# Moving the tiles at the upper end of SBUF by 416 bytes, padding the rows of the transform operands, and keeping the probability tiles 32 bytes off

## The chip, the cores and the metric

The kernel runs on one core of one Trainium2 chip. The metric is the device time of one execution in microseconds; the time before is the median of three runs, and one more execution was taken with the profiler.

## The reference, cut to what matters

Two sequences (`x_prompt`, `x_sample`) of 1024 tokens, 1024 wide, go through one layer, all in float32. Each token row is normalised and modulated, then projected once; four heads of latent attention and eight groups of a two-dimensional Fourier transform share that projection and one output projection. A SwiGLU network of width 2816 follows.

```python
def layer(x, c, ...):
    h = rmsnorm(x, g_mix) * (1.0 + sc1) + sh1
    z = h @ w_in
    q_lat, kv_lat, k_pe, f_in = z[..., :o1], z[..., o1:o2], z[..., o2:o3], z[..., o3:]
    y_mla = mla_group(q_lat, kv_lat, k_pe, g_q_lat, w_uq, g_kv_lat, w_ukv)
    y_four = fourier_group(f_in, w_four)
    mix = jnp.concatenate([y_mla, y_four], axis=-1) @ w_out
    x = x + ga1 * mix
    h2 = rmsnorm(x, g_ffn) * (1.0 + sc2) + sh2
    ffn = (jax.nn.silu(h2 @ w_gate) * (h2 @ w_up)) @ w_down
    return x + ga2 * ffn
```

The result of each sequence is `rmsnorm(layer(x, c), g_final)`.

## The kernel before, in words

**The split product.** Nearly every product of two float32 matrices is made of three TensorE matmuls. Each operand is cut into a high part in the type float32r and the remainder: `split` (L63, L64) writes the high part with ScalarE and the remainder with VectorE. `mm3` (L79 to L81) then issues three matmuls into the same accumulator:

```python
nc.tensor.matmul(out, lh, rh, ...)   # L79
nc.tensor.matmul(out, lh, rl, ...)   # L80
nc.tensor.matmul(out, ll, rh, ...)   # L81
```

The second argument is the stationary operand, 128 columns that are loaded into the array by a weight load of its own (PEld in the profile); the third is the moving operand, up to 512 columns that stream past it. While one matmul streams, the weights of the next are loaded: at 999.85 us of the span a matmul of L81 starts, at 999.86 us the weight load for the L79 that follows it. So TensorE reads two places of SBUF at a time, the moving operand of this matmul and the stationary operand of the next. In the profile a group `bank<-H,wl` names what goes in, in no fixed order of moving and stationary; the lines settle it.

**The stages, in order of time.** First the input projection and the modulation vectors; then the Fourier transform, with moving `wm` and `wn` and stationary `A`, `B` and `ny` (`dft` and `fourier_out`, L946 to L1046; `wm` and `wn` are weights, `A` and `B` the transforms over the sequence). Then attention, in items of one sequence s, one block b of 256 rows, one head h and one half u: `scores` (L1216 to L1220) streams `lat`, the stored latents of sequence s, past `qa` and `qp`; the probabilities `p` are turned by transposes (`flip_p`, L1244) and split into `pt`; `values` streams `pt`, 256 columns wide, past `ckv`; `out_proj` streams `wv` past `o`. The items run s = 0 first, then s = 1, and the same code serves both.

Then the SwiGLU network, one sequence after the other, with a seven-product scheme for two-by-two blocks. **Gate and up** (`prod` and `step`): for each of 22 column blocks seven products, each of four chunks of 128, each of three matmuls. The moving operand is `H`, the normalised input in high and low parts, which stays in SBUF; the stationary one is `wh` and `wl`, split from the weights as they arrive. That is 22 x 7 x 4 = 616 calls of `mm3` for one sequence, 1232 for both. **Down** (`prod2`): the moving and the stationary operand are both fresh splits, so both are `wh` and `wl` tiles; 572 calls of `mm3` in this form. The last product of the second sequence is made from splits that were prepared in the room of the old `H` tiles, so there both operands are called `H`: 44 calls.

**Where the tiles lie.** A tile pool takes room from the lower end of each SBUF partition or, with `side="right"`, from the upper end; a pool is closed and its room is used again. The pools at the upper end grow down from byte 229344 of the partition, which is 32 more than a multiple of 64. What is in them comes in rows whose sizes are multiples of 64, so almost everything there starts 32 bytes off a multiple of 64, while the pools at the lower end start on multiples of 64. The starts, in bytes from the beginning of the partition as the built program has them, are these (a slice of a tile that the matmuls use starts a multiple of 512 bytes later, except in `A` and in the input projection's `wcs`):

| tile | end | part it plays | start before | rest by 64 | start after | rest by 64 |
|---|---|---|---|---|---|---|
| `H` (first of them `H20`) | lower | moving in gate and up | 11840 | 0 | 11840 | 0 |
| `wh` | upper | stationary in gate and up; both in down | 151520 | 32 | 151104 | 0 |
| `wl` | upper | the same | 176096 | 32 | 175680 | 0 |
| `val` | upper | sums, products, sources of `split` | 202720 | 32 | 202304 | 0 |
| `lat` of s = 0 | lower | moving in scores | 69184 | 0 | 69184 | 0 |
| `lat` of s = 1 | upper | moving in scores | 106464 | 32 | 105984 | 0 |
| `qa` | lower | stationary in scores | 42560 | 0 | 42560 | 0 |
| `qp` | lower | stationary in scores | 24128 | 0 | 24128 | 0 |
| `p` | upper | stationary in L1244 (`ident`, rest 0, moves) | 94176 | 32 | 93696 | 0 |
| `pt` | upper | moving in `values` | 122848 | 32 | 122400 | 32 |
| `ckv` | lower | stationary in `values` | 48704 | 0 | 48704 | 0 |
| `wv` | upper | moving in `out_proj` | 155616 | 32 | 155200 | 0 |
| `o` | upper | stationary in `out_proj` | 188384 | 32 | 187968 | 0 |
| `B` | upper | stationary in the Fourier stage (its `wm` stays at 32) | 107200 | 0 | 106720 | 32 |

All `wh`, `wl` and `val` tiles have the rest that the table gives for the first, and so have all `H` tiles.

Of the kernel before, what the change touches and what calls it, by code (L numbers as in the profile page):

```python
# [12 lines left out]
F32 = mybir.dt.float32  # L13
F32R = mybir.dt.float32r
# [7 lines left out]
P = 128  # L22
# [20 lines left out]
NZC = NCOS + NNYQ  # L43
NZS = 256
NCS = NZC + NZS
NY2 = 2 * NNYQ
ZOW = 4
NTE = 258
NT = 514
NX = 2 * (NCOS + NNYQ)  # L50


@with_exitstack
def hybrid_encoder_kernel(ctx: ExitStack, tc: tile.TileContext, a: dict):
# [4 lines left out]
    def rd(t):  # L59
        return t.bitcast(F32)  # L60

    def split(hi, lo, src, eng=None):
        here["a"] = nc.scalar.copy(hi, src).ins  # L63
        here["v"] = (eng or nc.vector).tensor_tensor(out=lo, in0=src, in1=rd(hi), op=ALU.subtract).ins  # L64
# [18 lines left out]
    const = ctx.enter_context(tc.tile_pool(name="const", bufs=1))  # L83
    tiny = ctx.enter_context(tc.tile_pool(name="tiny", bufs=4))
    dram = ctx.enter_context(tc.tile_pool(name="dram", bufs=1, space=DRAM))

    ident = const.tile([P, P], F32, name="ident")
    make_identity(nc, ident)
# [65 lines left out]
    zp = zpool.enter_context(tc.tile_pool(name="zp", bufs=1, side="right", reuse_waits="tile"))  # L154
    zc = [zp.tile([P, 4, NZC], F32, name=f"zc{s}") for s in range(2)]
    zs = [zp.tile([P, 4, NZS], F32, name=f"zs{s}") for s in range(2)]
    zo = zp.tile([ZOW, NZC], F32, name="zo")
    zx = zp.tile([P, NX], F32, name="zx")
    nc.gpsimd.memset(zx, 0.0)

# [3 lines left out]
    with ExitStack() as st:  # L164
        p1b = st.enter_context(ExitStack())
        w2 = p1b.enter_context(tc.tile_pool(name="p1b", bufs=1, side="right", reuse_waits="tile"))
        w = st.enter_context(tc.tile_pool(name="p1", bufs=1, reuse_waits="tile"))
# [568 lines left out]
        def raw_tile(name):  # L736
            return wr.tile([P, NT], F32, tag="raw", name=name, bufs=8)

        for _ in range(8):
            raw_tile("raw")  # L740
        zxs = [wr.tile([P, NX], F32R, name=f"zx{i}") for i in range(2)]
        zn = [wr.tile([P, 4, NY2], F32R, name=f"zn{i}") for i in range(2)]
        tcor = wr.tile([P, NTE], F32R, name="tcor")
        tb[0] = [wr.tile([P, 2, NT], F32R, name=f"tb0{i}") for i in range(2)]
        raws = {}

        def table_load(k):
            for c in range(2):
                raws[k, c] = raw_tile("raw")
                nc.sync.dma_start(raws[k, c][:, : (NT, 512)[k]], a[("tcos", "tsin")[k]][:, c, :])  # L750

# [64 lines left out]
    S = {}  # L816
# [98 lines left out]
    with ExitStack() as st:  # L915
        early = st.enter_context(ExitStack())
        wa = early.enter_context(tc.tile_pool(name="p2a", bufs=1, reuse_waits="tile"))
        w = st.enter_context(tc.tile_pool(name="p2", bufs=1, side="right", reuse_waits="tile"))
        pp = st.enter_context(tc.tile_pool(name="p2_ps", bufs=1, space=PSUM, reuse_waits="tile"))

        def bank2(tag="b"):
            return pp.tile([P, 512], F32, tag=tag, name="bank", bufs=2 if tag == "d" else 6)
# [5 lines left out]
            bank2(tag)  # L928

        zh, wms = {}, {}  # L930
        nyt = w.tile([P, NT], F32R, name="ny")
        for i in range(2):
            w.tile([P, 2, 512], F32R, tag=f"wm{i}10", name=f"wm{i}10", bufs=1)
        w.tile([P, 512], F32R, tag="wn1", name="wn1", bufs=1)
        nc.gpsimd.tensor_scalar(out=nyt, in0=ident[:, 0:1].broadcast_to([P, NT]), scalar1=0.0, scalar2=None, op0=ALU.mult).ins

# [8 lines left out]

        def dft(s, mid=None):  # L946
            z = zh.pop(s)
            A = [w.tile([P, 2, NT], F32R, tag=f"A{i}", name=f"A{i}", bufs=1) for i in range(2)]
            B = [w.tile([P, 2, 512], F32R, tag=f"B{i}", name=f"B{i}", bufs=1) for i in range(2)]
            if s == 0:  # L950
                wn0 = prep_wn(0, 0, wm1[1])
                next(wn0)
            for q in (0, 2, 1) if s == 0 else (0, 1):
                m = NY2 if q == 2 else P
                sl = slice(P * q, P * q + P)
                zz = zn if q == 2 else [z[0][i][:, :, sl] for i in range(2)]
                x0 = 2 * NCOS if q == 2 else NCOS * s + P * q
                pe, po = (bank2("d" if q == 0 else "b") for _ in range(2))
                for c in range(2):
                    mm3(pe[:m, :NTE], zz[0][:, 2 * c, :], zz[1][:, 2 * c, :], tb[0][0][:, c, :NTE], tb[0][1][:, c, :NTE], c == 0, False)  # L960
                for c in range(2):
                    mm3(po[:m, :256], zz[0][:, 2 * c + 1, :], zz[1][:, 2 * c + 1, :],
                        tb[0][0][:, c, NTE:NT], tb[0][1][:, c, NTE:NT], c == 0, c == 1)
                for i in range(2):
                    nc.tensor.matmul(pe[:m, :NTE], zxs[i][:, x0 : x0 + m], tcor, start=False, stop=i == 1)
                if q == 2:
                    ah = w.tile([NY2, NT], F32R, name="nyh")
                    al = raw_tile("nyl")[:NY2]
                else:
                    ah, al = A[0][:, q, :], A[1][:, q, :]  # L970
                for o, v in ((slice(0, 256), pe[:m, :256]), (slice(256, 512), po[:m, :256]), (slice(512, 514), pe[:m, 256:NTE])):
                    split(ah[:, o], al[:, o], v)
                if q == 2:
                    nc.vector.tensor_scalar(out=al, in0=al, scalar1=cmask[:m, 1:2], scalar2=None, op0=ALU.mult)
                    nc.vector.scalar_tensor_tensor(out=nyt[:m], in0=rd(ah), scalar=cmask[:m, 0:1], in1=al,
                                                   op0=ALU.mult, op1=ALU.add)
            if s == 0:
                with behind():
                    here["ny"] = here["a"], here["v"]
                    halves = [wm0, wm_half(0, 0, 1, w, wm1[0])]  # L980
                    wms[0] = {0: (halves, next(wn0))}
            if mid:
                mid()
            for q in range(2):
                sl = slice(P * q, P * q + P)
                pb = bank2()
                for v in range(2):
                    ks = slice(256 * v, 256 * v + 256)
                    for c in range(2):
                        mm3(pb[:, ks], z[1][0][:, 2 * c + v, sl], z[1][1][:, 2 * c + v, sl],  # L990
                            tb[1][0][:, c, ks], tb[1][1][:, c, ks], c == 0, c == 1)
                split(B[0][:, q, :], B[1][:, q, :], pb)
            return A, B, nyt

        def prep_wn(s, g, wnr):
            wnh = w.tile([P, 512], F32R, tag="wnh", name="wnh", bufs=1)
            wn = w.tile([P, 512], F32R, tag=f"wn{g}", name=f"wn{g}", bufs=1)
            nc.scalar.copy(wnh, wnr)
            nc.gpsimd.tensor_tensor(out=wnr, in0=wnr, in1=rd(wnh), op=ALU.subtract)
            nc.gpsimd.tensor_scalar(out=wnr, in0=wnr, scalar1=cmask[:, 3 + 2 * s : 4 + 2 * s], scalar2=None, op0=ALU.mult)  # L1000
            yield
            nc.vector.scalar_tensor_tensor(out=wn, in0=rd(wnh), scalar=cmask[:, 2 + 2 * s : 3 + 2 * s], in1=wnr,
                                           op0=ALU.mult, op1=ALU.add)
            yield wn
# [17 lines left out]
        def fourier_out(s, ABn, j, g):  # L1022
            A, B, ny = ABn
            (wc, wd), wn = wms[s][g]
# [3 lines left out]
            for q in range(2):  # L1028
                mm3(pa, A[0][:, q, js], A[1][:, q, js], wc[0][:, q, :], wc[1][:, q, :], q == 0, False)
            nc.tensor.matmul(pa, ny[:, js], wn, start=False, stop=True)  # L1030
# [7 lines left out]
            if j == 0:  # L1038
                pn = bank2()
                for q in range(2):  # L1040
                    mm3(pn[:2, :], A[0][:, q, 512:514], A[1][:, q, 512:514], wc[0][:, q, :], wc[1][:, q, :], q == 0, False)
                nc.tensor.matmul(pn[:2, :], ny[:, 512:514], wn, start=False, stop=True)
# [159 lines left out]
    with ExitStack() as st:  # L1202
        w = st.enter_context(tc.tile_pool(name="p3", bufs=1, side="right", reuse_waits="tile"))
# [32 lines left out]
        def flip_p(s, b, h, u):  # L1236
            p = S.pop(("p", s, b, h, u))
            if u == 0:
                S["pt", s, b, h] = [w.tile([P, 8, 2, P], F32R, tag=f"pt{k}", name=f"pt{k}", bufs=2) for k in range(2)]
            pth, ptl = S["pt", s, b, h]  # L1240
            for g in range(2):
                pt = tbank("ppt")
                for c in range(4):
                    nc.tensor.transpose(pt[:, c, :], p[:, (4 * g + c) * P : (4 * g + c + 1) * P], ident)  # L1244
                split(pth[:, 4 * g : 4 * g + 4, u, :], ptl[:, 4 * g : 4 * g + 4, u, :], pt)
# [18 lines left out]
        def comb_h(s, c):  # L1264
            A = e.tile([P, 4, 512], F32, tag="lat00", name="hca")
            B = e.tile([P, 4, 512], F32, tag="lat01", name="hcb")
# [51 lines left out]
        for k in range(nit + 4):  # L1318
            if k >= nit:
                i = k - nit  # L1320
# [5 lines left out]
            if k < nit:  # L1326
# [3 lines left out]
                i = k % 8  # L1330
# [27 lines left out]
    with ExitStack() as st:  # L1358
        w = st.enter_context(tc.tile_pool(name="p5", bufs=1, reuse_waits="tile"))
# [162 lines left out]
        for s in range(2):  # L1522
# [78 lines left out]
            A = {}  # L1601
            late = None
            for n, f in enumerate(order):
# [78 lines left out]
                if n % 2 == 1:  # L1682
                    late = (n // 2, A)
                    A = {}
# [300 lines left out]
```

## Time and profile before

| | |
|---|---|
| runs | 2051.56, 2048.66, 2051.51 us; median 2051.51 us |
| profiled execution | 2051.31 us |
| its span, first to last instruction | 2049.5 us, so 1.8 us lie around it |
| TensorE busy | 2006.0 us, 98% of the span |
| granted TensorE clock, mean | 0.996 |

How to read it: the profile's page names a group of instructions by line, engine, operation and tiles, with the count, the busy time and the mean length of one. The length of a matmul in the records reaches from the start of its stream to a modelled end; consecutive matmuls overlap, so the time that each one takes out of the span is the distance between two starts, which the timeline shows.

### The profile page before, as it was taken

Reading aid. Unit: us, or ns where it says so; the run is one execution under the profiler, and the core shown is the slowest. Engines: PE = TensorE matmul, PEld = TensorE weight load, DVE = VectorE, ACT = ScalarE, POOL = GpSimd, SP = SyncE. Lnnn points to the kernel's source line nnn. Section 1 sums busy time; section 2 is a strip of 40 time slices with the busy share of each in tenths; the row PEclk is TensorE's granted clock in tenths of the full one; section 3 lists DMA queues with packets and bytes.
Section 4 is the critical chain, followed back from the end, with each engine's and each line's share of the span. In section 5 each row is a group of like instructions: output and inputs, shape, how many; then the busy total and the mean of one; then the engine's idle time right before and its main releaser. Section 6 shows DMA issues by size and latency. Waiting matters only on the chain.

```text
span 2049.5 us, 28369 instructions
## 1 busy us (share of the span) xinstructions
PE 2006.0 (98%) x9910; PEld 1641.6 (80%) x9910; DVE 1397.2 (68%) x2076; ACT 890.5 (43%) x1732; POOL 827.0 (40%) x972
## 2 busy tenths in 40 slices
PE   7899999999999999999999999999999999999998
PEld 3778778888888878888888888877888888888876
DVE  4568758666677778767777577688665665667585
ACT  2675436555555563333232365454323333336441
POOL 0564213112313237878878311234544444420142
PEclk9999999999999999999999999999999999999999
DMA  9786884444544475555455587674322322258662
GB/s 387 256 317 211 293 307 116 111 99 113 146 102 143 139 268 202 174 194 186 174 172 186 168 305 249 216 233 162 132 93 88 117 90 103 94 182 277 221 231 95
DMA packets 183036, 376.64 MB, mean 184 GB/s; under 512 B 17996, under 2 KB 57548, under 8 KB 179052
## 3 DMA queue, kind: packets, MB, share of 16 engines
q1 hardware_dynamic: 165548, 321.33, 45.9%
q0 software_dynamic: 17344, 53.49, 8.7%
q8 instruction: 78, 1.28, 0.2%
q14 instruction: 66, 0.54, 0.1%
HBM read 262.75 MB, written 120.39 MB: 187 GB/s over the span
## 4 chain that ended last, share of the span: by engine, by line
PE 55%; DVE 3%; DMA 2%; issue 1%; POOL 1%; ACT 0%; SPq 0%; DVEq 0%; ACTq 0%; POOLq 0%
PE bank L81 18%; PE bank L79 18%; PE bank L80 18%; DVE wl L64 1%; DVE val L137 1%; DMA draw<-s_d 1%; POOL val L137 0%; DMA val<-x_d 0%; DVE val L1782 0%; DMA draw<-t_d 0%; ACT wh L63 0%; DVE val L134 0%; POOL rs_y L105 0%; DVE H L64 0%; DMA rgu<-in_wgu_dram 0%
## 5 line engine op out<-in xcount | busy, mean ns | idle before, releaser
L79 PE MATMUL bank<-H,wh 128*128 128x512 f32 x1232 | 487.5, 396 | 2.4 <-DVE val L137 0.9
L81 PE MATMUL bank<-H,wl 128*128 128x512 f32 x1232 | 488.6, 397 | 0.2 <-DVE wl L64 0.2
L80 PE MATMUL bank<-H,wh 128*128 128x512 f32 x1232 | 484.4, 393 | 0.3 <-DVE H L64 0.3
L79 PEld LDWEIGHTS bank<-H,wh 128*128 128x128 f32 x1232 | 231.2, 188 | 58.6 <-DVE val L137 1.8
L80 PEld LDWEIGHTS bank<-H,wh 128*128 128x128 f32 x1232 | 231.3, 188 | 58.1 <-DVE H L64 0.6
L81 PEld LDWEIGHTS bank<-H,wl 128*128 128x128 f32 x1232 | 231.3, 188 | 56.9 <-DVE wl L64 0.5
L64 DVE TENSOR_TENSOR wl<-draw,wh 128x512 fp32r<-128x512 f32 x286 | 202.7, 743 | 85.6 <-ACT wh L63 85.2
L137 DVE TENSOR_TENSOR val<-bank,val 128x512 f32<-128x512 f32 x200 | 136.7, 689 | 158.8 <-PE bank L81 153.4
L63 ACT CAST wh<-draw 128x512 fp32r<-128x512 f32 x286 | 168.6, 619 | 159.3 <-PE bank L80 82.9
L137 POOL TENSOR_TENSOR val<-val 128x512 f32<-128x512 f32 x58 | 84.0, 1456 | 365.5 <-DVE val L1756 188.8
L80 PE MATMUL bank<-wl,wh 128*128 128x512 f32 x572 | 223.6, 391 | 2.3 <-DVE wl L64 2.3
L63 ACT CAST wh<-rgu 128x512 fp32r<-128x512 f32 x172 | 106.8, 621 | 269.5 <-PE bank L80 209.5
L81 PE MATMUL bank<-wh,wl 128*128 128x512 f32 x572 | 222.6, 389 | 0.0
L79 PE MATMUL bank<-wh 128*128 128x512 f32 x572 | 222.6, 389 | 0.0
L63 ACT CAST wh<-val 128x512 fp32r<-128x512 f32 x133 | 82.2, 621 | 269.8 <-PE bank L80 253.1
L64 DVE TENSOR_TENSOR wl<-val,wh 128x512 fp32r<-128x512 f32 x133 | 130.8, 985 | 77.3 <-ACT wh L63 77.3
L64 DVE TENSOR_TENSOR wl<-rgu,wh 128x512 fp32r<-128x512 f32 x172 | 166.8, 970 | 3.7 <-ACT wh L63 3.7
L134 POOL TENSOR_TENSOR val<-rgu 128x512 f32<-128x512 f32 x80 | 117.7, 1472 | 100.9 <-DMA rgu<-in_wgu_dram 97.2
L80 PEld LDWEIGHTS bank<-wl,wh 128*128 128x128 f32 x572 | 107.3, 188 | 27.4 <-DVE wl L64 5.4
L79 PEld LDWEIGHTS bank<-wh 128*128 128x128 f32 x572 | 107.4, 188 | 22.4
L81 PEld LDWEIGHTS bank<-wh,wl 128*128 128x128 f32 x572 | 107.4, 188 | 22.2
L1225 DVE TENSOR_REDUCE mx<-ps_s 128x1 f32<-128x1024 f32 x64 | 78.2, 1222 | 61.3 <-PE ps_s L1220 60.9
(385 smaller groups left out, 4048.4 us busy)
## 6 DMA issues: line engine op xcount, KB each, us to landing
rgu<-in_wgu_dram SPq DMA_DIRECT2D x86, 512.0 KB, 4.4
draw<-s_d SPq DMA_DIRECT2D x143, 256.0 KB, 3.8
s_d<-val POOLq DMA_DIRECT2D x88, 256.0 KB, 3.9
draw<-t_d SPq DMA_DIRECT2D x88, 256.0 KB, 4.2
s_d<-val SPq DMA_DIRECT2D x66, 256.0 KB, 2.4
draw<-in_w_down_dram SPq DMA_DIRECT2D x55, 256.0 KB, 4.6
wada<-in_w_ada_dram SPq DMA_DIRECT2D x11, 1024.0 KB, 10.5
xt<-in_x_dram SPq DMA_DIRECT2D x16, 512.0 KB, 10.3
```

The costliest lines, as they stand in the source:

```text
L63: here["a"] = nc.scalar.copy(hi, src).ins
L64: here["v"] = (eng or nc.vector).tensor_tensor(out=lo, in0=src, in1=rd(hi), op=ALU.subtract).ins
L79: nc.tensor.matmul(out, lh, rh, start=first, stop=False, skip_group_check=cont)
L80: nc.tensor.matmul(out, lh, rl, start=False, stop=False, skip_group_check=cont)
L81: here["t"] = nc.tensor.matmul(out, ll, rh, start=False, stop=last, skip_group_check=cont).ins
L134: return eng.tensor_tensor(out=out, in0=x, in1=y, op=ALU.subtract).ins
L137: eng.tensor_tensor(out=out, in0=x, in1=y, op=ALU.add)
L1225: nc.vector.tensor_reduce(out=mx, in_=ps, axis=AX.X, op=ALU.max)
```

## The change

- A tile `edge` of 104 floats (416 bytes) in a pool of its own is taken first at the upper end. No instruction touches it. Every later pool at the upper end starts 416 bytes lower, an odd multiple of 32.
- `zo` gets 8 more floats behind its row, so what is allocated below it in the first stages moves by 448 bytes, a multiple of 64, and keeps its rest.
- `ny`, `A` and `nyh` get rows of 528 instead of 514 floats (2112 bytes, a multiple of 64, instead of 2056); the instructions use the first 514, as before.
- Before the first pair of `pt` tiles a tile of 32 bytes is allocated, and another after it, so that `pt` keeps its rest of 32 and the tiles behind it come to rest 0.

No instruction is added, removed or put elsewhere: TensorE has the same 8932 rows in the same order before and after, VectorE the same 1682, and so on for each engine. The waits are the same as well, but for one: the fill of `ny` on GpSimd no longer waits for an earlier matmul, since its new place doesn't overlap what that matmul read.

```diff
+NTP = 528
...
+    edge = ctx.enter_context(tc.tile_pool(name="edge", bufs=1, side="right"))
+    edge.tile([P, 104], F32, name="edge")
...
-    zo = zp.tile([ZOW, NZC], F32, name="zo")
+    zo = zp.tile([ZOW, NZC + 8], F32, name="zo")[:, :NZC]
...
-        nyt = w.tile([P, NT], F32R, name="ny")
+        nyt = w.tile([P, NTP], F32R, name="ny")[:, :NT]
...
-            A = [w.tile([P, 2, NT], F32R, tag=f"A{i}", name=f"A{i}", bufs=1) for i in range(2)]
+            A = [w.tile([P, 2, NTP], F32R, tag=f"A{i}", name=f"A{i}", bufs=1)[:, :, :NT] for i in range(2)]
...
-                    ah = w.tile([NY2, NT], F32R, name="nyh")
+                    ah = w.tile([NY2, NTP], F32R, name="nyh")[:, :NT]
...
             if u == 0:
+                if not S.get("gap"):
+                    w.tile([P, 8], F32, name="gap0")
                 S["pt", s, b, h] = [w.tile([P, 8, 2, P], F32R, tag=f"pt{k}", name=f"pt{k}", bufs=2) for k in range(2)]
+                if not S.get("gap"):
+                    S["gap"] = w.tile([P, 8], F32, name="gap1")
```

## The prediction

> **What bounds the kernel now.** First the page: the share of each engine, and the clock in 40 slices.
>
> ```profile
> span 2049.5 us, 28369 instructions
> ...
> PE 2006.0 (98%) x9910; PEld 1641.6 (80%) x9910; DVE 1397.2 (68%) x2076; ACT 890.5 (43%) x1732; POOL 827.0 (40%) x972
> ...
> PEclk9999999999999999999999999999999999999999
> ```
>
> TensorE has hardly a gap and its clock is full all along. A busy TensorE is not yet one that works at its best, so the next question is how far apart its matmuls stand. Before that, the stages: three stretches cut out of gate and up of the first sequence, down of the first, and gate and up of the second. Columns: length, busy time and count for PE, PEld, DVE, ACT and POOL, granted clock, DMA share, GB/s.
>
> ```profile
> 780.00:1180.00 400.00, 400.00 (x1716) 321.75 (x1716) 283.97 (x287) 121.59 (x204) 301.37 (x274) 1.00 0.52 178
> 1200.00:1410.00 210.00, 208.56 (x915) 171.03 (x914) 156.06 (x231) 110.34 (x205) 43.16 (x56) 1.00 0.71 239
> 1430.00:1830.00 400.00, 399.51 (x1713) 321.11 (x1712) 239.97 (x290) 122.28 (x206) 181.16 (x156) 1.00 0.30 105
> ```
>
> In gate and up TensorE is busy for 400.00 of 400 us and 399.51 of 400, with VectorE at 284 and 240 and GpSimd at 301 and 181. Nothing but TensorE sets the length of these stages. Now the groups by form: gate and up (`H` with `wh` or `wl`), down (`wh` and `wl` alone, two of its three lines), and the last product of down, where both operands are `H`.
>
> ```profile
> L81 PE MATMUL bank<-H,wl 128*128 128x512 f32 x1232 | 488.6, 397 | 0.2 <-DVE wl L64 0.2
> L79 PE MATMUL bank<-H,wh 128*128 128x512 f32 x1232 | 487.5, 396 | 2.4 <-DVE val L137 0.9 <-ACT H L63 0.6 <-DVE val L1662 0.5
> L80 PE MATMUL bank<-H,wh 128*128 128x512 f32 x1232 | 484.4, 393 | 0.3 <-DVE H L64 0.3
> L80 PE MATMUL bank<-wl,wh 128*128 128x512 f32 x572 | 223.6, 391 | 2.3 <-DVE wl L64 2.3
> L81 PE MATMUL bank<-wh,wl 128*128 128x512 f32 x572 | 222.6, 389 | 0.0
> ...
> L81 PE MATMUL bank<-H 128*128 128x512 f32 x44 | 17.1, 389 | 0.0
> L80 PE MATMUL bank<-H 128*128 128x512 f32 x44 | 17.1, 389 | 0.0
> L79 PE MATMUL bank<-H 128*128 128x512 f32 x44 | 17.1, 389 | 0.0
> ```
>
> The reader is to see that the same three matmuls, equal in shape and type, take 397 + 396 + 393 = 1186 ns in gate and up and 3 x 389 = 1167 ns in the last product, a difference of 19 ns for each call of `mm3`. The idle column says that it is no wait: 2.9 us for all 3696 matmuls of gate and up. These lengths reach over the next matmul's start; the timeline shows what one costs. Gate and up first, then the last product:
>
> ```profile
> 1000.09 0.39 PE L79 MATMUL bank<-H,wh 128*128 128x512 f32 x1
> ...
> 1001.49 0.39 PE L79 MATMUL bank<-H,wh 128*128 128x512 f32 x1
> ```
>
> ```profile
> 2019.92 0.39 PE L79 MATMUL bank<-H 128*128 128x512 f32 x1
> ...
> 2021.96 0.39 PE L79 MATMUL bank<-H 128*128 128x512 f32 x1
> ```
>
> Two calls of `mm3` in 1.40 us against three in 2.04 us: 0.70 us and 0.68 us a call. The 19 ns are real spacing.
>
> **What tells the two kinds apart.** By the table of starts, `H` has rest 0 by 64 and `wh` and `wl` have rest 32: in gate and up the moving operand and the stationary operand that is loaded meanwhile differ by 32. In down both have rest 32, in the last product both have rest 0, and both are quick. Attention holds the same comparison on equal code: `scores` streams `lat` past `qa` and `qp` (rest 0), and `lat` has rest 0 for the first sequence (301 to 504 us) and rest 32 for the second (505.4 to 715.3 us).
>
> ```profile
> L1216 PE MATMUL ps_s<-lat,qa 128*128 128x512 f32 x64 | 26.4, 413 | 0.0
> L1218 PE MATMUL ps_s<-lat,qa 128*128 128x512 f32 x64 | 25.3, 395 | 0.0
> L1217 PE MATMUL ps_s<-lat,qa 128*128 128x512 f32 x64 | 25.1, 393 | 0.0
> L1220 PE MATMUL ps_s<-lat,qp 128*128 128x512 f32 x64 | 25.1, 392 | 0.0
> L1219 PE MATMUL ps_s<-lat,qp 128*128 128x512 f32 x64 | 25.1, 392 | 0.0
> ```
>
> ```profile
> L1216 PE MATMUL ps_s<-lat,qa 128*128 128x512 f32 x64 | 26.9, 420 | 0.5 <-DVE p L1232 0.5
> L1218 PE MATMUL ps_s<-lat,qa 128*128 128x512 f32 x64 | 25.6, 400 | 0.9 <-DVE qa L64 0.9
> L1217 PE MATMUL ps_s<-lat,qa 128*128 128x512 f32 x64 | 25.5, 399 | 0.0
> L1219 PE MATMUL ps_s<-lat,qp 128*128 128x512 f32 x64 | 25.3, 396 | 0.0
> L1220 PE MATMUL ps_s<-lat,qp 128*128 128x512 f32 x64 | 25.3, 396 | 0.0
> ```
>
> All five lines are slower in the second sequence: 2011 ns against 1985 ns, 26 ns for five matmuls or 5.2 ns each, beside 19 / 3 = 6.3 ns each in gate and up. So I read: **equal rests are quick, rests that differ by 32 are slow.**
>
> The Trainium skill speaks against this. In "TensorE: Matmul & The Clock Gate", section "Step-by-step: what each phase is for", it gives TensorE two independent read ports of SBUF and says: "Loading the next tile's weights doesn't steal SBUF read bandwidth from the running matmul." By that rule the place of an operand could not matter, the sum below would be zero and the time 2051 us; the 26 ns between two passes of the same lines disagree with it, as far as one trace can; its outcome is that of rival 1.
>
> **The change part by part.** Durations come from the profiled execution, so the sum is made against its 2051.31 us (span 2049.5 and 1.8 around it); the median of the runs, 2051.51, stands 0.2 above.
>
> *Gate and up.* `wh` and `wl` go from rest 32 to rest 0, `H` stays at 0: all 3696 matmuls go from unlike to like. By the last product's rows, 1232 calls x 19 ns = **-23.4 us**. By the attention rows it would be 3696 x 5.2 ns = -19.2 us. I take the first, because it compares long unbroken runs with each other, as gate and up is; `scores` is broken up by shorter work (its 413 and 420 on the first line show it).
>
> *Scores.* `lat` of the second sequence goes to rest 0: 64 x 26 ns = **-1.7 us**.
>
> *Down and `out_proj`.* Both operands move from 32 to 0 together: like before, like after, **0**.
>
> *`values` and the input projection.* `pt` keeps 32 against `ckv` at 0, and the first stages move by 448 bytes, which changes no rest: **0**.
>
> *Fourier stage.* The 96 matmuls of `wm` and `B` become like.
>
> ```profile
> L79 PE MATMUL bank<-wm,B 128*128 128x512 f32 x32 | 12.7, 397 | 0.0
> ```
>
> Against 389 they could win 96 x 7 ns = 0.7 us; the runs are short, and of the matmuls with `A`, whose rests were mixed and whose second row stood 8 bytes off, about half end unlike. Ends: -1.0 and +0.5 us; I take **0**, between them.
>
> *Transposes of `p`.* The stationary operand goes from unlike to like.
>
> ```profile
> L1244 PE MATMUL ppt<-ident,p 128*128 128x128 f32 x512 | 69.9, 275 | 1.9 <-DVE p L1232 0.8 <-DVE nb L1226 0.6
> ...
> L522 PE MATMUL bank<-ident,lat 128*128 128x128 f32 x64 | 8.5, 273 | 3.4 <-DVE lat L498 3.4
> ```
>
> L522 has both at rest 0 and 273 ns. The ends are 512 x 2 ns = -1.0 us and, with the sign turned, +1.0; **0**, since so short a stream is near the same in both.
>
> *VectorE, ScalarE, GpSimd and the DMAs* work on the moved tiles too. VectorE's `split` by line, minimum, median and maximum in ns, sources and results at rest 32 first, at rest 0 second:
>
> ```profile
> L64 DVE TENSOR_TENSOR wl<-val,wh x133: 676/691/3495, 764.0 to 1804.7; 128x512 fp32r<-128x512 f32 x133
> ...
> L64 DVE TENSOR_TENSOR H<-H,H x58: 679/686/1850, 726.5 to 1881.6; 128x512 fp32r<-128x512 f32 x46, 128x1024 fp32r<-128x1024 f32 x12
> ```
>
> 691 and 686 are the same to 1%. Cost nothing: in gate and up 116 us of VectorE's 400 are free. If that cover were gone, TensorE's wait for `wl` would show it; today it is 0.2 us there. The stage shrinks by 23.4 of some 862 us (1232 x 0.70), 2.7%, so VectorE's share goes from 71% to 73% and GpSimd's from 75% to 77%: nothing is late next. The DMAs, at 0.52 and 0.30, are the same ones in the same order. GpSimd's fill of `ny`, without its wait, comes earlier and was waited for by no row above: 0.
>
> Sum: -23.4 - 1.7 = -25.1 us; 2051.3 - 25.1 = 2026.2, rounded to **2026 us**.
>
> **The rivals.** *(1) The place does not matter, or not the rest by 64.* Stages differ in more than addresses, and every unlike pair named so far, `B` apart, also has one operand from each end of SBUF, which the change leaves so. Then nothing moves: 2051 us. For it: the confusion of rest and end is real. Against it: the two gate-and-up stretches have very different GpSimd and DMA loads (301 and 181 us, 0.52 and 0.30) and the same count in 400 us (1716 and 1713); and `wm` and `B`, both at the upper end and unlike, stand at 397, not 389. Chance 0.09.
>
> *(2) Slower: the moving operand's own rest decides.* `H` at 0 would be slow, `wh` at 32 quick. The change then takes down from quick to slow, 572 x 19 ns = +10.9 us, and `out_proj`, whose `wv` also moves from 32 to 0, 128 calls x 19 ns = +2.4 us, and leaves gate and up: 2051.3 + 13.3 = 2065 us. It decides as soon as a moving `wh` at rest 0 takes over 0.69 us a call. Against it: a moving `H` at 0 runs at 389 in the last product, and `lat` at 0 is the quicker. Chance 0.04.
>
> *(3) A wait takes the gain's place.* With TensorE 2.7% quicker, GpSimd's sums in the first gate-and-up stretch (301 of 400) or down's loads could come late. If a fourth to all of the first sequence's 11.7 us went so, the time is 2029 to 2038 us. For it: down already waits 2.3 us for `wl`. Against it: no such wait within gate and up. Chance 0.07.
>
> **How the numbers follow.** The forecast has 0.80. Its own range: at the quick end -23.4 - 1.7 - 1.0 - 1.0 = -27.1, and the runs before reach 2.9 us below their median, so 2021; at the slow end -19.2 - 1.7 + 1.5 = -19.4, 2032. To 2033 it takes in the better part of the third rival, and 0.2 is left out with the first two and the rest of the third. A measurement of this kernel can tell some 0.2%, 4 us, from no change. Faster: 0.80 + 0.07 = 0.87; same: 0.09; slower: 0.04.
>
> **What would show it.** Right: the three `H` groups at about 389 each and 0.68 us between every third start; L1216 to L1220 alike in both sequences; the `wh` groups of down still at 389 to 391; `pt` groups as before; TensorE's idle time in gate and up still under 5 us. Wrong: `H` groups still at 393 to 397 (rival 1), `wh` groups of down at 393 or more (rival 2), or idle time before L79 to L81 with `wl` or `val` as releaser (rival 3).

## The result, and the profile after

| | before | after |
|---|---|---|
| median of four runs | 2051.53 us (2048.66 to 2051.96) | 2027.78 us (2025.50 to 2029.65) |
| profiled execution | 2051.31 us | 2027.96 us |

The ratio is 0.9881, with a 95% interval from 0.9869 to 0.9894: 1.2% faster. The forecast was 2026 us.

The page first: span, share of the engines, and the clock in 40 slices, after the change.

```profile
span 2026.1 us, 28369 instructions
...
PE 1978.9 (98%) x9910; PEld 1640.5 (81%) x9910; DVE 1399.9 (69%) x2076; ACT 891.0 (44%) x1732; POOL 827.2 (41%) x972
...
PEclk9999999999999999999999999999999999999999
```

The same counts (9910 matmuls, in the same order of tiles in both traces; the 8932 and 1682 rows named under "The change" are another count than the page's), the same clock, and 27.1 us less of busy TensorE (2006.0 to 1978.9). Its idle time grew by 3.7 us, from 43.5 to 47.2, so the span is shorter by 23.4 us only. The other engines' busy time is within 3 us of before. Now the groups by form, after: busy time and mean ns of one, then idle time before them.

```profile
L80 PE MATMUL bank<-H,wh 128*128 128x512 f32 x1232 | 480.0, 390 | 3.3 <-DVE val L140 1.3 <-DVE val L1669 0.8 <-ACT H L64 0.7
L81 PE MATMUL bank<-H,wh 128*128 128x512 f32 x1232 | 479.5, 389 | 0.3 <-DVE H L65 0.3
L82 PE MATMUL bank<-H,wl 128*128 128x512 f32 x1232 | 479.3, 389 | 0.2 <-DVE wl L65 0.2
L81 PE MATMUL bank<-wl,wh 128*128 128x512 f32 x572 | 223.7, 391 | 3.4 <-DVE wl L65 3.4
L82 PE MATMUL bank<-wh,wl 128*128 128x512 f32 x572 | 222.7, 389 | 0.0
L80 PE MATMUL bank<-wh 128*128 128x512 f32 x572 | 222.6, 389 | 0.0
L80 PE MATMUL gb<-pt,ckv 128*128 128x256 f32 x256 | 73.8, 288 | 0.0
L82 PE MATMUL gb<-pt,ckv 128*128 128x256 f32 x256 | 72.9, 285 | 0.0
L81 PE MATMUL gb<-pt,ckv 128*128 128x256 f32 x256 | 72.7, 284 | 0.0
```

The three `H` groups went from 1186 to 390 + 389 + 389 = 1168 ns, within a nanosecond of the 1167 that the last product had before; down and `pt` stand where they stood. The timeline of after at the place that the prediction showed:

```profile
1000.49 0.39 PE L80 MATMUL bank<-H,wh 128*128 128x512 f32 x1
...
1001.85 0.39 PE L80 MATMUL bank<-H,wh 128*128 128x512 f32 x1
```

Two calls of `mm3` in 1.36 us instead of 1.40. What the two stages took is read from the first and the last start of this line's matmuls with `H` in each sequence (count, ns minimum, median and maximum, then first and last start). Before:

```profile
L79 PE MATMUL bank<-H,wh x616: 391/392/505, 748.0 to 1183.5; 128*128 128x512 f32 x154
...
L79 PE MATMUL bank<-H,wh x616: 392/399/499, 1396.3 to 1828.4; 128*128 128x512 f32 x154
```

After:

```profile
L80 PE MATMUL bank<-H,wh x616: 387/389/503, 746.4 to 1171.0; 128*128 128x512 f32 x154
...
L80 PE MATMUL bank<-H,wh x616: 389/389/504, 1384.8 to 1805.0; 128*128 128x512 f32 x154
```

The first stage went from 435.5 to 424.6 us, the second from 432.1 to 420.2: together -22.8 us. The four starts cut the whole span: ahead of the first gate and up -1.6 us (748.0 to 746.4), between the two +1.0 (212.8 to 213.8), behind the second 0.0 (221.1 both times). -22.8 - 1.6 + 1.0 = -23.4, which is the whole difference of the spans. The gain is where the prediction put it.

One sign did not come. These are the five lines of `scores` after, in the second sequence (503.3 to 714 us):

```profile
L1219 PE MATMUL ps_s<-lat,qa 128*128 128x512 f32 x64 | 26.7, 418 | 0.5 <-DVE p L1235 0.5
L1221 PE MATMUL ps_s<-lat,qa 128*128 128x512 f32 x64 | 25.6, 400 | 1.0 <-DVE qa L65 1.0
L1220 PE MATMUL ps_s<-lat,qa 128*128 128x512 f32 x64 | 25.4, 396 | 0.0
L1223 PE MATMUL ps_s<-lat,qp 128*128 128x512 f32 x64 | 25.3, 395 | 0.0
L1222 PE MATMUL ps_s<-lat,qp 128*128 128x512 f32 x64 | 25.2, 394 | 0.0
```

They take 2003 ns, hardly less than the 2011 before, while the first sequence takes 411 + 391 + 392 + 391 + 392 = 1977 in the same run. That first sequence itself took 1985 ns before, though neither its `lat` nor its `qa` moved, so 8 ns between two kernels can come from something else. `lat` and `qa` of the second sequence now both have rest 0 by 64, and the lines are still slow. So "equal rests by 64 are quick" cannot be the whole rule, and the experiments are about what the rule is.

### The profile page after: what moved, and what is told of

Its sections match the earlier page's. It is cut to its first block, busy times and chain, and to the rows that moved or that the text cites. A ratio compares the mean times of both kernels' runs of the same rounds, so it can differ in the third digit from the quotient of the medians.

```text
span 2026.1 us, 28369 instructions
## 1 busy us (share of the span) xinstructions
PE 1978.9 (98%) x9910; PEld 1640.5 (81%) x9910; DVE 1399.9 (69%) x2076; ACT 891.0 (44%) x1732; POOL 827.2 (41%) x972
## 4 chain that ended last, share of the span: by engine, by line
PE 54%; DVE 4%; DMA 2%; issue 1%; POOL 1%; ACT 1%; SPq 0%; DVEq 0%; ACTq 0%; POOLq 0%
PE bank L81 18%; PE bank L80 18%; PE bank L82 18%; DVE wl L65 2%; DVE val L140 1%; DMA draw<-s_d 1%; DMA draw<-t_d 1%; DVE val L1789 0%; ACT wh L64 0%; DVE val L137 0%; DMA X<-hc_d 0%; POOL val L140 0%; POOL rs_y L108 0%; DVE val L1778 0%; DVE val L1763 0%
## 5 line engine op out<-in xcount | busy, mean ns | idle before, releaser
L80 PE MATMUL bank<-H,wh 128*128 128x512 f32 x1232 | 480.0, 390 | 3.3 <-DVE val L140 1.3
L81 PE MATMUL bank<-H,wh 128*128 128x512 f32 x1232 | 479.5, 389 | 0.3 <-DVE H L65 0.3
L82 PE MATMUL bank<-H,wl 128*128 128x512 f32 x1232 | 479.3, 389 | 0.2 <-DVE wl L65 0.2
L65 DVE TENSOR_TENSOR wl<-rgu,wh 128x512 fp32r<-128x512 f32 x172 | 171.0, 994 | 3.8 <-ACT wh L64 3.8
L65 DVE TENSOR_TENSOR wl<-val,wh 128x512 fp32r<-128x512 f32 x133 | 126.1, 950 | 64.4 <-ACT wh L64 64.3
L137 POOL TENSOR_TENSOR val<-rgu 128x512 f32<-128x512 f32 x80 | 112.7, 1409 | 92.9 <-DMA rgu<-in_wgu_dram 89.2
```

The source lines that it names most:

```text
L80: nc.tensor.matmul(out, lh, rh, start=first, stop=False, skip_group_check=cont)
L81: nc.tensor.matmul(out, lh, rl, start=False, stop=False, skip_group_check=cont)
L82: here["t"] = nc.tensor.matmul(out, ll, rh, start=False, stop=last, skip_group_check=cont).ins
L137: return eng.tensor_tensor(out=out, in0=x, in1=y, op=ALU.subtract).ins
```

## The experiments

Every matmul in question streams a moving operand while a stationary one is loaded. What the theories differ in is which property of the two addresses sets the distance between matmuls.

- **A**, the prediction's: the rests by 64 are equal or not.
- **B**: equality is needed by a larger power of two.
- **R**, B with its figure, formed after the first four runs: what counts is the difference, moving minus stationary, by 256.
- **C**: `scores` of the second sequence is slow for a reason that is not its addresses.
- **D**: for the 256-column streams (`pt`), 32 bytes off is better than even, which would be a reason for the small tiles around `pt`.
- **S**: not the difference counts, but the place of `wh` and `wl` itself.

The starts in the table ahead of the prediction give the differences. `H` minus `wh` is 11840 - 151520 = -139680, or 96 by 256 (-546 x 256 + 96); 416 bytes lower it is -139264 = -544 x 256, or 0. `lat` of the first sequence minus `qa` is 69184 - 42560 = 104 x 256, or 0; of the second sequence 160 before and 192 after. `wh` against `wl` in down is 24576 = 96 x 256, or 0.

In the table below the H groups are the mean lengths of the three lines in ns. The distance is the mean from one start to the next of these matmuls in gate and up, worked out from the starts in the records, distances over 250 ns left out (for `pt`, further below, over 150). The times of before and after are medians of four, the others of one profiled execution; the kernel before, beside them on the same chips, had medians of 2055.15, 2053.73 and 2052.17 us.

| run | bytes put in | `H` minus `wh`, by 256 | H groups, ns | distance, ns | time, us |
|---|---|---|---|---|---|
| before | - | 96 | 396, 393, 397 | 233.3 | 2051.53 |
| after | 416 upper | 0 | 390, 389, 389 | 226.7 | 2027.78 |
| edge160 | 160 upper | 0 | 390, 389, 389 | 226.7 | 2024.81 |
| lower416 | 416 lower | 0 | 390, 389, 389 | 226.7 | 2028.36 |
| edge192 | 192 upper | 32 | 396, 395, 395 | 233.3 | 2050.45 |
| edge224 | 224 upper | 64 | 393, 392, 391 | 228.9 | 2039.59 |
| edge288 | 288 upper | 128 | 395, 395, 395 | 232.8 | 2051.04 |
| edge352 | 352 upper | 192 | 396, 396, 396 | 233.3 | 2050.36 |
| edge384 | 384 upper | 224 | 396, 396, 396 | 233.3 | 2053.49 |

One more rival has no letter. What `H` meets at the upper end could be the traffic of another engine, since `val` and the splits that VectorE and ScalarE write lie there and move with `wh`. The traces speak against it. Before, 99.9% of the 3680 distances are 230 ns or more, so nearly every matmul is late, and the 160 of them with VectorE, ScalarE and GpSimd all idle from 300 ns before a start to 300 ns after it average 233.3 ns like the rest; after, 142 such distances average 226.7 ns. The DMAs don't show either: the two sequences, with a DMA share of 0.52 and 0.30, both have 233.3 ns before.

**1. Other sizes of `edge`, all even by 64.** 352, 288 and 160 bytes are odd multiples of 32 like 416, so all three give `wh` rest 0 by 64.

```diff
-    edge.tile([P, 104], F32, name="edge")
+    edge.tile([P, 88], F32, name="edge")
```

> The changed kernel with an edge of 352 instead of 416 bytes: in gate and up the stationary tiles now stand 64 bytes off H by 512 (rest by 64 still equal), lat of the second sequence stands exactly like qa by 512. Theory A (only the rest by 64 counts): the H groups stay at 389 ns, time about 2028 us, scores of the second sequence unchanged at 2003 ns for the five lines. Theory B (equality by a larger power of two is needed, 128 or more): H groups back at 393 to 397, scores of the second sequence down to about 1977 ns as in the first, time 2049 to 2051 us. Theory C (scores of the second sequence are slower for reasons other than addresses): scores stay at 2003 ns whatever gate and up does.

Groups by form of edge352:

```profile
L80 PE MATMUL bank<-H,wh 128*128 128x512 f32 x1232 | 487.6, 396 | 2.3 <-DVE val L140 0.9 <-ACT H L64 0.7 <-DVE val L1669 0.5
L81 PE MATMUL bank<-H,wh 128*128 128x512 f32 x1232 | 487.3, 396 | 0.3 <-DVE H L65 0.3
L82 PE MATMUL bank<-H,wl 128*128 128x512 f32 x1232 | 487.1, 396 | 0.2 <-DVE wl L65 0.2
```

Together they take 1188 ns, against 1186 before, and the time is 2050.36 us. This kernel has every other part of the change and equal rests by 64, and the whole gain is gone: A falls. In the same run `lat` of the second sequence lies 64 bytes higher than in the changed kernel, so its difference to `qa` is 0 by 256 instead of 192. Its five lines (503.3 to 716 us):

```profile
L1219 PE MATMUL ps_s<-lat,qa 128*128 128x512 f32 x64 | 26.6, 415 | 0.5 <-ACT qa L64 0.5
L1221 PE MATMUL ps_s<-lat,qa 128*128 128x512 f32 x64 | 25.4, 397 | 1.0 <-DVE qa L65 1.0
L1220 PE MATMUL ps_s<-lat,qa 128*128 128x512 f32 x64 | 25.3, 395 | 0.0
L1222 PE MATMUL ps_s<-lat,qp 128*128 128x512 f32 x64 | 25.1, 392 | 0.0
L1223 PE MATMUL ps_s<-lat,qp 128*128 128x512 f32 x64 | 25.0, 391 | 0.0
```

1990 ns against 2003, and the two lines with `qp` at 392 and 391, as in the first sequence. The runs further below agree: 1986 to 1990 ns in all six in which this difference is 0, 1995 at 64 (edge288), and 2003 to 2011 at every other. So C falls too: gate and up and `scores` answer to the same kind of difference, one becoming slow and the other quick by the same 64 bytes.

```diff
-    edge.tile([P, 104], F32, name="edge")
+    edge.tile([P, 72], F32, name="edge")
```

> Edge of 288 bytes: in gate and up moving and stationary operand stand 128 bytes apart by 512. Theory A (rest by 64): H groups at 389, 2028 us. Theory B with 128 as the power that must agree: 389 and 2028; B with 256 or 512: 393 to 397 and about 2050.

Slow again (395, 395, 395; 2051.04 us), at a difference of 128: equality by 64 or by 128 is not enough. The first of its lines:

```profile
L80 PE MATMUL bank<-H,wh 128*128 128x512 f32 x1232 | 486.9, 395 | 2.4 <-DVE val L140 1.0 <-ACT H L64 0.7 <-DVE val L1669 0.5
```

```diff
-    edge.tile([P, 104], F32, name="edge")
+    edge.tile([P, 40], F32, name="edge")
```

> Edge of 160 bytes: 256 bytes apart by 512 in gate and up. Theory A: 389, 2028 us. Theory B with 128 or 256: 389, 2028; B with 512 (or only the exact same place by more than that): 393 to 397, 2050 us.

Quick (390, 389, 389), 2024.81 us, with `H` minus `wh` at 256 by 512. So equality by 512 is not needed, and as far as the value at 0 tells, 256 bytes is the period. The first of its lines:

```profile
L80 PE MATMUL bank<-H,wh 128*128 128x512 f32 x1232 | 479.9, 390 | 3.8 <-DVE val L1669 1.4 <-DVE val L140 1.3 <-ACT H L64 0.7
```

**2. The change without the tiles around `pt`.**

```diff
             if u == 0:
-                if not S.get("gap"):
-                    w.tile([P, 8], F32, name="gap0")
                 S["pt", s, b, h] = ...
-                if not S.get("gap"):
-                    S["gap"] = w.tile([P, 8], F32, name="gap1")
```

> The changed kernel without the two 32-byte tiles around pt: pt then stands like ckv by 512 (instead of 32 off), lat of the second sequence like qa (instead of 64 off); gate and up as in the changed kernel, 389. Theory A: the 768 matmuls of pt turn from unlike to like and gain (at most 768 x 6 ns = 4.6 us), scores unchanged; 2023 to 2028 us. Theory B: scores of the second sequence 26 ns less for five lines, -1.7 us, pt gains as well or stays; 2022 to 2026 us. Rival D (a 256-column stream is best when it is off by 32): pt groups above 288, 285, 284 by some ns, +1 to +5 us, 2027 to 2033 us.

2029.22 us (2028.13 to 2030.72), ratio to before 0.9876 [0.986, 0.9893]: the two small tiles carry none of the gain that a measurement can see. The time is above what A and B expected and in D's range. The `pt` groups, now with a difference of 0 to `ckv`, are 1 or 2 ns longer each:

```profile
L80 PE MATMUL gb<-pt,ckv 128*128 128x256 f32 x256 | 74.1, 289 | 0.0
L82 PE MATMUL gb<-pt,ckv 128*128 128x256 f32 x256 | 73.4, 287 | 0.0
L81 PE MATMUL gb<-pt,ckv 128*128 128x256 f32 x256 | 73.1, 285 | 0.0
```

For streams of 256 columns 0 is thus not the best difference. By the starts in the records `pt` stands 119.4 ns apart at 0, 118.35 at after's 224: 768 x 1.05 ns = 0.8 us that the tiles save. Since they also put `lat` of the second sequence at 192 instead of 0, they lose about as much in `scores`, whose five lines take 1987 ns in this run against 2003: 64 x 16 ns = 1.0 us.

**3. The same difference from the other end.** Nothing of the change is made; 416 bytes are put in at the lower end, so `H` and what else lies above them there (`qa`, `qp`, `ckv`, `lat` of the first sequence) move up, and `wh` and `wl` stay at 32 by 64.

```diff
+    const.tile([P, 104], F32, name="low")
```

> The kernel before with 416 bytes taken at the lower end instead: H moves to the rest that wh and wl have by 256 (224), which stay where they were. Theory R (what counts is the difference between the moving operand and the stationary one that is loaded meanwhile, by 256): H groups at 389 to 390, time 2025 to 2030 us, scores alike in both sequences at about 1980 to 1990 ns for the five lines. Rival S (the place of wh and wl itself counts): H groups at 393 to 397, about 2050 us.

Groups by form of lower416:

```profile
L79 PE MATMUL bank<-H,wh 128*128 128x512 f32 x1232 | 479.9, 390 | 4.0 <-DVE val L1663 1.7 <-DVE val L138 1.4 <-ACT H L63 0.7
L80 PE MATMUL bank<-H,wh 128*128 128x512 f32 x1232 | 479.5, 389 | 0.3 <-DVE H L64 0.3
L81 PE MATMUL bank<-H,wl 128*128 128x512 f32 x1232 | 479.3, 389 | 0.2 <-DVE wl L64 0.2
```

The whole gain (2028.36 us), though `wh`, `wl`, `val` and all the rest of the upper end lie where they lay before, and off a multiple of 64. S falls, and with it any theory in which an even place is better for itself: what lower416 and after have in common is the difference. `scores` took 1980 and 1989 ns in the two sequences, alike as R expected.

**4. The other differences.** Three more sizes fill the circle.

```diff
-    edge.tile([P, 104], F32, name="edge")
+    edge.tile([P, 48], F32, name="edge")
```

> Edge of 192 bytes: H stands 32 bytes after wh by 256. Theory R, with the points 0: 227, 64: 230 (scores in edge288), 96: 233 ns so far, gives 228 to 230 ns of spacing, groups 391 to 392, time 2031 to 2039 us. If every difference other than 0 is slow alike: 233 ns, groups 395, 2050 us.

A difference of 32: slow (396, 395, 395; 2050.45 us). R had expected 228 to 230 ns and 2031 to 2039 us, as if the distance rose little by little from 0; 233.3 ns came, so that part of R failed. The first of its lines:

```profile
L80 PE MATMUL bank<-H,wh 128*128 128x512 f32 x1232 | 487.1, 396 | 2.4 <-DVE val L140 1.0 <-ACT H L64 0.7 <-DVE val L1669 0.5
```

```diff
-    edge.tile([P, 104], F32, name="edge")
+    edge.tile([P, 56], F32, name="edge")
```

> Edge of 224 bytes: H stands 64 bytes after wh by 256. Theory R with the point of scores (64: 230 ns): groups 392 to 393, time 2036 to 2041 us, so between the two kernels. If every difference is slow alike: groups 395, 2050 us.

A difference of 64 is a case of its own. Groups by form of edge224:

```profile
L80 PE MATMUL bank<-H,wh 128*128 128x512 f32 x1232 | 483.6, 393 | 3.7 <-DVE val L140 1.3 <-DVE val L1669 1.0 <-ACT H L64 0.7
L81 PE MATMUL bank<-H,wh 128*128 128x512 f32 x1232 | 482.8, 392 | 0.3 <-DVE H L65 0.3
L82 PE MATMUL bank<-H,wl 128*128 128x512 f32 x1232 | 481.1, 391 | 0.2 <-DVE wl L65 0.2
```

1176 ns lies between 1168 and 1186, and so does the time, 2039.59 us. The starts of gate and up confirm that it is the stage:

```profile
L80 PE MATMUL bank<-H,wh x616: 388/394/501, 749.3 to 1178.4; 128*128 128x512 f32 x154
...
L80 PE MATMUL bank<-H,wh x616: 392/392/502, 1391.2 to 1815.8; 128*128 128x512 f32 x154
```

429.1 + 424.6 = 853.7 us, 8.9 more than after's 844.8; another 2.9 us came ahead of the stage (749.3 against 746.4), a start that lies between 744.3 and 749.3 us over all these runs.

```diff
-    edge.tile([P, 104], F32, name="edge")
+    edge.tile([P, 96], F32, name="edge")
```

> Edge of 384 bytes: H stands 224 after wh by 256, that is 32 before it. Theory R with the points 32: 233.3, 96: 233.3, 192: 233.4 ns gives 232 to 234 ns, groups 395, 2049 to 2052 us. If a distance of 32 in this direction is as good as none (the direction counts): groups 389 to 391, 2028 to 2035 us.

A difference of 224, 32 on the other side of 0: slow (396, 396, 396; 2053.49 us). The first of its lines:

```profile
L80 PE MATMUL bank<-H,wh 128*128 128x512 f32 x1232 | 487.7, 396 | 3.1 <-DVE val L140 1.3 <-DVE val L1669 1.0 <-ACT H L64 0.7
```

With 0 quick and all else slow, R holds but for 64, and 64 is not mirrored by 192, which is slow.

**5. Better places for `pt` and `lat`.** If the difference by 256 counts, the small tiles can be chosen for `pt` and for `lat` of the second sequence together.

```diff
-                    S["gap"] = w.tile([P, 8], F32, name="gap1")
+                    S["gap"] = w.tile([P, 56], F32, name="gap1")
```

> The changed kernel with the tile after pt grown from 32 to 224 bytes: lat of the second sequence comes to difference 0 by 256 against qa, pt to 32 after ckv, gate and up stay at 0. Theory R and the points measured (scores 233.0 to about 229, pt 118.35 to 117.04 ns): 320 x 3.7 = 1.2 us and 768 x 1.3 = 1.0 us less than the changed kernel, 2024 to 2028 us; five score lines of the second sequence at about 1987 ns, pt groups at 287, 283, 284. If scores or pt are slow for other reasons: no change, 2026 to 2029 us, 2004 ns and 288, 284, 285.

`lat` at 0 and `pt` at 32: 2027.41 us (2024.52 to 2028.04), ratio 0.9862 [0.9844, 0.988]. The `pt` groups are 287, 284 and 283, a nanosecond less than after, and `scores` took 1988 ns instead of 2003. R made this 2.2 us less than the changed kernel; 0.4 came, which is not told apart from nothing, and from the first to the last L1219 attention took 411.7 us against after's 411.5 (below). TensorE's idle time in that stretch was 6.2 us against 4.9, so waits took part of the gain; the transposes' wait for VectorE's `p` rose from 0.9 to 2.3 us. D holds so far as 32 beats 0 here (116.9 ns apart against 119.4), but 192 beats both, as the next run shows.

```diff
-                    w.tile([P, 8], F32, name="gap0")
+                    w.tile([P, 48], F32, name="gap0")
...
-                    S["gap"] = w.tile([P, 8], F32, name="gap1")
+                    S["gap"] = w.tile([P, 16], F32, name="gap1")
```

> The changed kernel with 192 bytes ahead of pt and 64 behind it: pt stands 192 after ckv by 256 (the quickest place so far, 115.2 ns in edge192), lat of the second sequence at difference 0, gate and up at 0. Theory R: against the changed kernel 768 x 3.1 = 2.4 us and 320 x 3.7 = 1.2 us less, 2023 to 2025 us beside after_again at 2027 to 2029; pt groups 286, 282, 283. If the 115.2 came from something else in edge192: pt stays at 288, 284, 285 and only 1.2 us go.

`lat` at 0 and `pt` at 192, the place at which edge192 had shown 286, 283 and 282. `scores` of the second sequence (503.3 to 714 us), then `pt`, in gap192_64:

```profile
L1219 PE MATMUL ps_s<-lat,qa 128*128 128x512 f32 x64 | 26.5, 414 | 0.5 <-ACT qa L64 0.5
L1221 PE MATMUL ps_s<-lat,qa 128*128 128x512 f32 x64 | 25.3, 396 | 1.0 <-DVE qa L65 1.0
L1220 PE MATMUL ps_s<-lat,qa 128*128 128x512 f32 x64 | 25.2, 394 | 0.0
L1222 PE MATMUL ps_s<-lat,qp 128*128 128x512 f32 x64 | 25.0, 391 | 0.0
L1223 PE MATMUL ps_s<-lat,qp 128*128 128x512 f32 x64 | 25.0, 391 | 0.0
```

```profile
L80 PE MATMUL gb<-pt,ckv 128*128 128x256 f32 x256 | 73.2, 286 | 0.0
L82 PE MATMUL gb<-pt,ckv 128*128 128x256 f32 x256 | 72.3, 283 | 0.0
L81 PE MATMUL gb<-pt,ckv 128*128 128x256 f32 x256 | 72.1, 282 | 0.0
```

Both moved as R has it: 1986 ns for the five lines instead of 2003, and 2 ns less for each `pt`. In time, attention from its first to its last L1219 took, after:

```profile
L1219 PE MATMUL ps_s<-lat,qa x128: 388/394/502, 301.0 to 712.5; 128*128 128x512 f32 x128
```

and in gap192_64:

```profile
L1219 PE MATMUL ps_s<-lat,qa x128: 388/392/504, 302.0 to 710.6; 128*128 128x512 f32 x128
```

411.5 and 408.6 us, 2.9 us less. The whole time, 2026.87 us (2024.15 to 2031.55), misses the 2023 to 2025 us that R expected, and is not told apart from the changed kernel's on the same chip:

> The changed kernel once more, on the same chip as the others: 2026 to 2029 us, all theories alike.

No edit; 2028.26 us (2027.55 to 2028.82), ratio 0.988 [0.9865, 0.9894], H groups 390, 389, 389, and 411.2 us for the same stretch of attention. The version that the experiments point to is better in its stage and not shown to be better in all.

**6. Only the `edge`.** The kernel before with the one tile, without the padded rows and the small tiles.

```diff
+    edge = ctx.enter_context(tc.tile_pool(name="edge", bufs=1, side="right"))
+    edge.tile([P, 104], F32, name="edge")
```

> The kernel before with the edge of 416 bytes alone, without padded rows, the longer zo and the tiles around pt. Gate and up at difference 0, scores of both sequences at 0, pt at 0 (119.4 ns). Theory R: 2027 to 2029 us, so the edge carries the whole gain; five score lines of the second sequence at about 1988 ns, pt groups 289, 285, 287. If the padding of A, ny and zo is worth something: above 2029 us, with the matmuls on A, B and ny longer than in the changed kernel.

2029.81 us (2028.62 to 2032.96), ratio 0.989 [0.9874, 0.9907], H groups 390, 389, 389. The range overlaps that of after_again, and the medians stand 1.55 us apart, so the 416 bytes carry the gain, and what the rest adds is about that at most and not shown. The Fourier groups hold next to nothing of it: with `wm` and `A` 416, 398, 394 in after_again and 415, 397, 394 here, with `wm` and `B` 398, 393, 394 and 398, 395, 395, each of 32 matmuls.

## Why the prediction was right, point by point, and where it was not

**What bounds it: right.** Gate and up was all TensorE, its matmuls stood too far apart, and when they closed up the time followed one for one: 22.8 of 23.4 us.

**"Equal rests are quick, rests that differ by 32 are slow": the step that failed.** It named the right pair, the moving operand and the stationary one, and the right relation, equality, but the wrong modulus. edge352 and edge288 have equal rests by 64 and are slow, edge224 has them and is in between; the modulus that fits is 256. The trace of before could not decide between 64 and 256, since its quick pairs differ by 0 and its slow ones by 96 and 160. But the table of starts gave whole addresses, and I cut them to their rest by 64 without asking by which power of two the quick pairs agree: they agree by 256. With 352 bytes in place of 416 the forecast would have been as sure, and the time 2050.36 us. The outcome was right for gate and up because 416 fits both rules, and as far as the prediction's reasons go, that was luck.

**Gate and up, -23.4 us: right.** -22.8 measured; of the two prices, that of the last product (19 ns a call) was the right one and that of `scores` (-19.2 us) too low, perhaps because `scores` is broken by shorter work.

**Scores, -1.7 us: wrong by that step.** Its difference went from 160 to 192, from slow to slow; 64 x 8 ns = -0.5 us came, no more than the first sequence lost with its difference unchanged (1985 to 1977). In edge352 and gap192_64, where it is 0, 13 and 17 ns a pass came beside after.

**Down, `out_proj`, `values`, transposes: right at 0.** 391, 389, 389 for down in both kernels, and the `pt` groups within 1 ns. For down and `out_proj` the difference is 0 before and after; `pt` went from 160 to 224, 118.2 and 118.35 ns apart. It was costed at nothing because its rest stays; it does so because these two happen to be alike, as 192 (115.2) is not.

**Fourier stage, 0 between -1.0 and +0.5: nothing seen.** `wm` with `B` was predicted to become like, and by 64 it did; by 256 its difference went from 32 to 64. 397, 395, 395 became 398, 393, 394.

**No wait takes the gain: nearly.** The third rival had 2029 us and more. Idle time before the `H` groups rose from 2.9 to 3.8 us, before `wl` with `wh` from 2.3 to 3.4, with VectorE's `val` and `wl` as the main releasers, and the stretch between the two stages, where the first down lies, took 1.0 us longer. Over the whole span 3.7 us of idle time were added.

**The Trainium skill's two independent ports** ("TensorE: Matmul & The Clock Gate", "Step-by-step: what each phase is for"), by which, as the prediction reads them, place could not matter: here it does, and more clearly than in the trace of before. With the same instructions, lower416 and edge352 differ by 6.6 ns in the distance of `H` matmuls and by 22 us, and only in where tiles lie. The first rival, which was that outcome, falls with both its halves: not the end of SBUF (`H` is still lower and `wh` upper), and not the rest by 64, but an address all the same. The second rival, the moving operand's own rest, falls with down's 391 and 389.

**The sum.** Forecast 2026.2, profiled 2027.96. By the four starts: 0.6 us of the gap is gate and up, 1.0 the stretch with down, 0.1 the part ahead. That part ahead gave -1.6 where -1.7 was forecast, but not from the forecast's cause alone: -0.5 from each sequence's `scores` is in it, and the first `lat` matmul started 0.8 us earlier (301.8 to 301.0), which no step foresaw. In the other kernels that start lies between 299.3 and 303.8 us, so I read nothing into it.

**What stays open.** The runs show that the difference by 256 counts, not what in the chip makes it so. In gate and up the stationary operand loaded meanwhile and the one that the stream itself uses have the same rest, so which of the two is the partner was not tried apart; nor was the reason why 64 is nearly quick and 192 slow. `scores` of the first sequence, whose difference is 0 in every run, stands between 228.3 and 230.7 ns apart, so something else is worth up to 2.4 ns there; what it is was not tried.

## What to carry to other kernels

Where TensorE is busy without a gap, compare the mean length of groups that are equal in shape and type: a few ns between them, times 3696 matmuls, were worth 22.8 us here, while TensorE's idle time before these matmuls was 2.9 us in all. Then write down the whole addresses of the pair that TensorE reads at a time, and ask by which power of two the quick pairs agree, before an alignment is chosen; one or two sizes of an untouched tile test it. A rule that is read from one trace fits every modulus at which its examples agree, so the forecast should carry the larger ones as rivals.

## What the runs showed of the hardware that was not expected

- Distance of 512-column matmuls by the difference of moving and stationary operand by 256 bytes, in gate and up: 226.7 ns at 0, 228.9 at 64, and 232.8 to 233.3 at 32, 96, 128, 192 and 224. In `scores` of the second sequence, broken by other work: 228.6 to 229.8 at 0, 230.3 at 64, 232.3 to 233.7 at 128, 160, 192 and 224; in the first sequence, always at 0, 228.3 to 230.7.
- With 256 columns (`pt` past `ckv`) the best difference of the six that were met is another: 115.2 ns at 192, 116.9 and 117.0 at 32, 118.2 and 118.35 at 160 and 224, 119.3 to 119.5 at 0 and 119.8 at 96.
- An untouched tile of 416 bytes, and nothing else, is worth 1.1% of this kernel at the upper end of SBUF (onlyedge) and 1.2% at the lower (lower416, one execution); one of 384 bytes at the upper end, with the rest of the change, is worth nothing (edge384).
